# A hybrid decoder trunk on one core: parameter transfers held back behind the first unit of weights, and skip factors loaded as rows

## The chip, the core and the metric

The kernel runs as one program on one core of one Trainium2 chip. The metric is the device time of one execution in microseconds (us). The time before is the median of three runs.

## The reference, cut to what matters

Two decoder layers over 256 tokens of width 1024, all in float32. Each layer adds a mixer and a feed-forward part to the running activations, each behind an RMSNorm. The mixer projects the normed activations with `w_in` (1024 x 3592) into three groups: a short gated convolution, a state-space group (SSD, eight heads of 64) and a conformer convolution of 31 taps. What touches the change is the SSD group and the order of its small parameters:

```python
proj = h @ w_in
dt = softplus(s_dt + dt_bias)          # s_dt: 8 of the columns of proj
a = -exp(a_log)
y_s = ssd_chunked(xh, dt, a, ...)
y_s = y_s + d_skip[:, None] * xh       # one factor per head and layer
y_s = gated_rmsnorm(y_s, s_z, ssd_norm_w)
```

The feed-forward part is a dense SwiGLU in layer 0 and, in layer 1, two of eight SwiGLU experts per token, chosen by a router. A last RMSNorm ends the work.

## The kernel before, in words

Weights come from memory as a list of units, each a tile `raw` of about 2 MB, through a ring of four buffers (later nine). `Stream.load_upto` issues their transfers on SyncE's queue (SP below), in the order of the list. A unit is used in pieces: for each piece ScalarE rounds it to `whi` (line 235), VectorE forms the rest `wlo` (line 236), and TensorE runs three matmuls per block of 128 rows (`mm3`, lines 409 to 411: `whi` with `xh`, `whi` with `xl`, `wlo` with `xh`). Pieces are made four ahead of their use. Unit 0, 512 columns of `w_in`, is loaded in four quarters of 512 KB, one per piece (the branch `FINE`, line 200), each with runs of 512 bytes; the other mixer units come in one transfer (line 202) with runs of 2 KB.

At the start ACT loads one row tile, and SP issues `x` in four quarters (line 277), then the four quarters of unit 0, then eight rows of parameters of layer 0 (`prow_load(0)`, line 302), then units 1, 2, 3. TensorE transposes `x` (line 333); ScalarE and VectorE copy it to `xT` and split it, scaled, into `xh` and `xl` (lines 418, 419).

GpSimd (POOL) issues the other small parameters on its own queue as soon as the program starts, lines 306 to 317: `dtb` and `alg` (the same 16 floats to every partition), `wdt` for each layer (eight columns of `w_in`: 1024 runs of 32 bytes), two row sets into `prow2`, `dsk` in two halves (64 partitions x 8 single floats, 4 bytes each, picked by stride so that each half of the partitions holds the factors of its heads), eight rows of layer 1 (`prow_load(1)`) and the router weights `wr`. Their users are: `na` = exp of `alg` (line 529, ScalarE), `wdh` and `wdl`, the split of `wdt` (lines 371 and 372), `dtv` (line 556), `ys` with `dsk` (line 634), and `load_rest` (from line 377) with `prow2`, `prow1` and `wr`.

SP issues in the written order (`MANUAL`); ScalarE, VectorE and TensorE do so at the very start, and later a scheduler sets their order. An engine runs its instructions in that order: one that waits holds all behind it.

Of the kernel before, what the change touches and what calls it, by code (L numbers as in the profile page):

```python
# [8 lines left out]
F32 = mybir.dt.float32  # L9
# [6 lines left out]
P = 128  # L16
T = 256
D = 1024
KD = D // P
# [14 lines left out]
HC = DFE // 2  # L34
LW = HC // 4
HB = HC // P
MANUAL = {mybir.EngineType.SP}


@with_exitstack  # L40
def hybrid_decoder(
# [6 lines left out]
    nc = tc.nc  # L48
    ACT, DVE, PE, POOL = nc.scalar, nc.vector, nc.tensor, nc.gpsimd
# [7 lines left out]
    work = t1.enter_context(tc.tile_pool(name="work", bufs=1))  # L57
    ctx.enter_context(tc.manual_schedule(engines=MANUAL))

# [7 lines left out]
    units = []  # L67
# [181 lines left out]
    ws = Stream()  # L249
# [32 lines left out]
    prow2 = work.tile([12, P], F32, name="prow2")  # L282
    COL = {}
    wdt = work.tile([P, 2, KD, 8], F32, name="wdt")
    wdh = work.tile([P, 2, KD, 8], F32R, name="wdh")
    wdl = work.tile([P, 2, KD, 8], F32R, name="wdl")
    dtb = work.tile([P, 2, 8], F32, name="dtb")
    alg = work.tile([P, 2, 8], F32, name="alg")
    dsk = work.tile([P, 2, 4], F32, name="dsk")
    wr = const.tile([P, KD, E], F32, name="wr")  # L290

    def bcast(ap, dims):
        return bass.AP(tensor=ap.tensor, offset=ap.offset, ap=[[0, P]] + dims)

    def prow_load(i):
        r = 0
        for nm, ap, n in (("conf", conv_conf_w[i].rearrange("k c -> (k c)"), 62),
                          ("conv_ssd", conv_ssd_w[i].rearrange("k c -> (k c)"), 32),
                          ("ssd_b", conv_ssd_b[i], 8), ("norm_mix", norm_mix[i], 8), ("norm_ffn", norm_ffn[i], 8),
                          ("conv_a", conv_a_w[i].rearrange("k c -> (k c)"), 6),  # L300
                          ("conf_b", conv_conf_b[i], 2), ("ln_g", conf_ln_g[i], 2)):
            (nc.gpsimd if i else nc.sync).dma_start(prow[i][r:r + n], ap.rearrange("(r c) -> r c", c=P))
            COL[nm] = r
            r += n

    nc.gpsimd.dma_start(dtb, bcast(dt_bias, [[8, 2], [1, 8]]))
    nc.gpsimd.dma_start(alg, bcast(a_log, [[8, 2], [1, 8]]))
    for i in range(2):
        nc.gpsimd.dma_start(wdt[:, i], w_in[i, :, 2304:2312].rearrange("(k p) n -> p k n", p=P))
    nc.gpsimd.dma_start(prow2[0:4], conf_ln_b.rearrange("l (r c) -> (l r) c", c=P))  # L310
    nc.gpsimd.dma_start(prow2[4:12], ssd_norm_w.rearrange("l (r c) -> (l r) c", c=P))
    for h in range(2):
        nc.gpsimd.dma_start(dsk[h * 64:(h + 1) * 64],
                            bass.AP(tensor=d_skip.tensor, offset=d_skip.offset + h,
                                    ap=[[0, 64], [8, 2], [2, 4]]))
    prow_load(1)
    nc.gpsimd.dma_start(wr, moe_router[0].rearrange("(k p) n -> p k n", p=P))

    pc = [work.tile([P, P], F32, name=f"pc{i}") for i in range(2)]
    pc2 = work.tile([P, 12], F32, name="pc2")  # L320
# [2 lines left out]
    def col(i, nm, j):  # L323
        if nm == "ln_b":
            return pc2[:, 2 * i + j:2 * i + j + 1]
        if nm == "ssd_norm":
            return pc2[:, 4 + 4 * i + j:5 + 4 * i + j]
        if nm == "norm_mix" and i == 0:
            return pcn[:, j:j + 1]
        return pc[i][:, COL[nm] + j:COL[nm] + j + 1]  # L330
# [85 lines left out]
    def scaled_split(i, nm, j, xh, xl):  # L416
        w = col(i, nm, j)
        ACT.activation(xh[:, j], xT[:, j], AF.Copy, scale=w)
        DVE.scalar_tensor_tensor(xl[:, j], xT[:, j], w, xh[:, j].bitcast(F32), op0=OP.mult, op1=OP.subtract)
# [396 lines left out]
    for j in range(KD):  # L816
        if j == 1:
            ws.make_upto(1)
            prow_load(0)
        scaled_split(0, "norm_mix", j, xh, xl)  # L820
    start_pe.close()
    ws.make_upto(2)
# [325 lines left out]
    for q in range(NS):  # L1148
        e, h = divmod(q, 2)
# [178 lines left out]
```

## Time and profile before

| | |
|---|---|
| three runs | 1308.5, 1310.47, 1310.91 us; median 1310.47 |
| profiled execution | 1314.7 us, span 1312.8 us |
| TensorE busy | 1218.4 us (93%) |
| VectorE, ScalarE, GpSimd busy | 464.2, 266.0, 12.2 us |
| transfers | 424.01 MB, mean 323 GB/s |
| GpSimd's queue (software) | 688 packets, 0.72 MB, 0.7% of 16 engines' span |
| SyncE's queue | 90452 packets, 421.09 MB, 80.9% |

The span is the profiled stretch; the execution's own time is 1.9 us longer. Busy shares are averages over stages with different limits, so the page alone does not say what a microsecond at the start is worth. In the page's 40 slices TensorE stands at nine tenths or more in nearly all but the first, where it has four.

### The profile page before, as it was taken

The page shows a single profiled execution, that of the slowest core. Times are in us where ns is not written, and L with a number is a line of the kernel's source. Part 1 is how long each engine was busy: PE and PEld are TensorE (multiplying, and loading weights), DVE is VectorE, ACT ScalarE, POOL GpSimd, SP SyncE. Part 2 cuts the span into 40 slices and gives each one's busy share as a digit, 9 for nine tenths or more (in the row PEclk, how much of TensorE's full clock was granted, in tenths as well). Part 3 has the DMA queues.
Part 4 walks back from the last instruction along what each step waited for, and adds up shares of the span by engine and source line. Part 5 has one row for each costly group of instructions (what it writes and reads, how often), then busy time and mean ns, then how long its engine had stood idle before and what let it go on. Part 6 is the DMA issues. An engine that isn't in the chain of part 4 may idle for free. (4 is left out here: it accounts for less than half of the span.)

```text
span 1312.8 us, 28824 instructions
## 1 busy us (share of the span) xinstructions
PE 1218.4 (93%) x12994; PEld 792.9 (60%) x12994; DVE 464.2 (35%) x948; ACT 266.0 (20%) x446; POOL 12.2 (1%) x34
## 2 busy tenths in 40 slices
PE   4999999999999899999999999999999997897794
PEld 3997999999998734454444544545635533343242
DVE  3898765556898411101201111111020121020213
ACT  3671544444670300000000000100000000000001
POOL 3000000000000000000000000000000000000000
PEclk9999999999999899999999999999999999999997
DMA  7852465555252799999999999999999999999993
GB/s 157 300 193 65 161 205 183 191 193 193 97 185 73 316 371 384 381 411 420 422 417 422 419 410 422 417 422 420 418 422 418 418 422 417 421 420 418 420 357 121
DMA packets 91303, 424.01 MB, mean 323 GB/s; under 512 B 4590, under 2 KB 33493, under 8 KB 83476
## 3 DMA queue, kind: packets, MB, share of 16 engines
q1 hardware_dynamic: 90452, 421.09, 80.9%
q0 software_dynamic: 688, 0.72, 0.7%
q8 instruction: 122, 2.00, 0.6%
q14 instruction: 25, 0.20, 0.0%
q10 hardware_dynamic: 16, 0.00, 0.0%
HBM read 420.74 MB, written 1.05 MB: 321 GB/s over the span
## 5 line engine op out<-in xcount | busy, mean ns | idle before, releaser
L1034 PE MATMUL psA<-raw,xe 128*32 128x448 f32 x5024 | 485.8, 541 | 25.3 <-DMA raw<-in_moe_w_gate_dram 9.7
L1034 PEld LDWEIGHTS psA<-raw,xe 128*32 128x32 f32 x5024 | 180.7, 110 | 319.8 <-issue 286.5
L1078 PE MATMUL psB<-raw,ht 128*32 128x256 f32 x4296 | 240.7, 380 | 18.8 <-DMA raw<-in_moe_w_down_dram 10.7
L1078 PEld LDWEIGHTS psB<-raw,ht 128*32 128x32 f32 x4296 | 151.6, 110 | 108.5 <-issue 18.3
L409 PE MATMUL psB<-xh,whi 128*128 128x256 f32 x608 | 173.1, 285 | 0.0
L411 PE MATMUL psB<-xh,wlo 128*128 128x256 f32 x608 | 172.5, 284 | 0.0
L410 PE MATMUL psB<-xl,whi 128*128 128x256 f32 x608 | 172.2, 283 | 0.0
L236 DVE TENSOR_TENSOR wlo<-raw,whi 128x1024 fp32r<-128x1024 f32 x110 | 134.0, 1223 | 59.8 <-ACT whi L235 59.7
L235 ACT CAST whi<-raw 128x1024 fp32r<-128x1024 f32 x110 | 114.8, 1048 | 114.3 <-PE psB L410 51.9
L1054 ACT ACTIVATE sg<-psA 128x448 f32<-128x448 f32 x48 | 24.5, 542 | 476.7 <-PE psA L1034 466.7
L409 PEld LDWEIGHTS psB<-xh,whi 128*128 128x128 f32 x608 | 116.6, 192 | 0.7 <-issue 0.7
L411 PEld LDWEIGHTS psB<-xh,wlo 128*128 128x128 f32 x608 | 116.5, 192 | 0.2
L410 PEld LDWEIGHTS psB<-xl,whi 128*128 128x128 f32 x608 | 116.5, 192 | 0.1
L1066 DVE TENSOR_TENSOR pr<-psA,sg 128x448 f32<-128x448 f32 x48 | 43.0, 922 | 203.5 <-PE psA L1034 203.5
L1104 DVE STREAM_TRANSPOSE yt<-yc 128x256 f32<-128x256 f32 x24 | 9.7, 431 | 234.7 <-ACT yc L1102 234.4
L693 PE MATMUL psA<-yf,raw 128*128 128x256 f32 x256 | 62.2, 399 | 5.4 <-ACT yf L733 3.0
L693 PEld LDWEIGHTS psA<-yf,raw 128*128 128x128 f32 x256 | 49.7, 199 | 13.5 <-ACT yf L733 3.5
L1018 DVE COPY xe<-psC 128x384 f32<-128x384 f32 x8 | 4.5, 558 | 149.0 <-PE psC L1016 149.0
L540 DVE SCALAR_TENSOR_TENSOR conv<-gp,pc,conv 128x256 f32<-128x256 f32 x120 | 50.8, 476 | 0.0
L410 PE MATMUL psA<-al,whi 128*128 128x256 f32 x176 | 49.8, 283 | 0.0
L411 PE MATMUL psA<-ah,wlo 128*128 128x256 f32 x176 | 49.7, 282 | 0.0
L409 PE MATMUL psA<-ah,whi 128*128 128x256 f32 x176 | 49.3, 280 | 0.0
(285 smaller groups left out, 879.7 us busy)
## 6 DMA issues: line engine op xcount, KB each, us to landing
raw<-in_moe_w_gate_dram SPq DMA_DIRECT2D x64, 1792.0 KB, 25.5
raw<-in_moe_w_up_dram SPq DMA_DIRECT2D x64, 1792.0 KB, 23.9
raw<-in_moe_w_down_dram SPq DMA_DIRECT2D x30, 2048.0 KB
raw<-in_moe_w_down_dram SPq DMA_DIRECT2D x30, 1536.0 KB, 24.4
raw<-in_w_in_dram SPq DMA_DIRECT2D x9, 2048.0 KB, 14.0
raw<-in_ffn_w_gate_dram SPq DMA_DIRECT2D x11, 1024.0 KB, 5.4
raw<-in_ffn_w_up_dram SPq DMA_DIRECT2D x11, 1024.0 KB, 8.0
raw<-in_ffn_w_down_dram SPq DMA_DIRECT2D x5, 2048.0 KB, 9.0
```

Source lines behind the costliest of these rows:

```text
L235: ACT.copy(hi, raw)
L236: DVE.tensor_tensor(lo, raw, hi.bitcast(F32), op=OP.subtract)
L409: PE.matmul(ps, lhsT=hi, rhs=xh, start=start, stop=False, **kw)
L410: PE.matmul(ps, lhsT=hi, rhs=xl, start=False, stop=False, **kw)
L411: PE.matmul(ps, lhsT=lo, rhs=xh, start=False, stop=stop, **kw)
L540: DVE.scalar_tensor_tensor(conv[:, c], src, w, conv[:, c], op0=OP.mult, op1=OP.add)
L693: PE.matmul(acc[j][:, a], lhsT=raw[:, k, w], rhs=yf[b][:, k], start=(b + k == 0 and a == 0), stop=(b + k == 4), skip_group_check=True)
L1034: PE.matmul(banks[t][32 * j:32 * j + 32, 0:LW], lhsT=x[:, k, 32 * t:32 * t + 32], rhs=raw[:, k % 2, LW * j:LW * j + LW], start=(k == 0), s ...
L1054: ACT.activation(sg[:, t], bg[t][:, 0:LW], AF.Silu)
L1066: DVE.tensor_tensor(pr[:, t], by(bu[t][:, 0:LW]), by(sg[:, t]), op=OP.mult)
L1078: PE.matmul(psd[t // 2][32 * j:32 * j + 32, 256 * (t % 2):256 * (t % 2) + 256], lhsT=ht[:, t, b], rhs=w[:, j], start=(h == 0 and b == 0 an ...
L1104: DVE.transpose(yt[:, :, 32 * t:32 * t + 32], yc[:, t].rearrange("p (n c) -> p n c", c=32))
```

## The change

`MANUAL` now holds GpSimd too, so that its instructions run in the written order. All of its parameter transfers move into a function `late_params`, called after SP's `prow_load(0)` has been written. It begins with a GpSimd copy, `gate`, that reads the last element of unit 0's tile: GpSimd cannot go on before the last quarter of unit 0 has landed. `alg` now stands ahead of `dtb`. The two strided loads of `dsk` become one load of 16 floats to every partition (`dsall`) and, at the end, two GpSimd copies that pick every second column.

```diff
-MANUAL = {mybir.EngineType.SP}
+MANUAL = {mybir.EngineType.SP, mybir.EngineType.Pool}
...
+    dsall = work.tile([P, 2, 8], F32, name="dsall")
...
-    nc.gpsimd.dma_start(dtb, bcast(dt_bias, [[8, 2], [1, 8]]))
-    nc.gpsimd.dma_start(alg, bcast(a_log, [[8, 2], [1, 8]]))
-    for i in range(2):
-        nc.gpsimd.dma_start(wdt[:, i], w_in[i, :, 2304:2312].rearrange("(k p) n -> p k n", p=P))
...
-    for h in range(2):
-        nc.gpsimd.dma_start(dsk[h * 64:(h + 1) * 64],
-                            bass.AP(tensor=d_skip.tensor, offset=d_skip.offset + h,
-                                    ap=[[0, 64], [8, 2], [2, 4]]))
-    prow_load(1)
-    nc.gpsimd.dma_start(wr, moe_router[0].rearrange("(k p) n -> p k n", p=P))
+    def late_params():
+
+        gate = work.tile([P, 1], F32, name="gate")
+        POOL.tensor_copy(gate, ws.raw[0][:, KD - 1, units[0]["n"] - 1:units[0]["n"]])
+        nc.gpsimd.dma_start(alg, bcast(a_log, [[8, 2], [1, 8]]))
+        nc.gpsimd.dma_start(dtb, bcast(dt_bias, [[8, 2], [1, 8]]))
+        for i in range(2):
+            nc.gpsimd.dma_start(wdt[:, i], w_in[i, :, 2304:2312].rearrange("(k p) n -> p k n", p=P))
+        nc.gpsimd.dma_start(dsall, bcast(d_skip, [[8, 2], [1, 8]]))
...
+        prow_load(1)
+        nc.gpsimd.dma_start(wr, moe_router[0].rearrange("(k p) n -> p k n", p=P))
+        for h in range(2):
+            POOL.tensor_copy(dsk[h * 64:(h + 1) * 64],
+                             dsall[h * 64:(h + 1) * 64].rearrange("p l (c h) -> p l c h", h=2)[:, :, :, h])
...
             prow_load(0)
+            late_params()
```

The order on GpSimd at the start, before (a row with x2 stands for two instructions):

```order
L259 IOTA jp 128x128
L279 IOTA before 128x64
L306 DMA dtb<-in_dt_bias_dram 128x16
L307 DMA alg<-in_a_log_dram 128x16
L309 DMA wdt<-in_w_in_dram 128x8x8 x2
...
L313 DMA dsk<-in_d_skip_dram 64x8x1 x2
...
L317 DMA wr<-in_moe_router_dram 128x8x8
L844 DMA wffn<-in_norm_ffn_dram 128x1024
```

And now, where lines below the change have moved by up to six:

```order
L259 IOTA jp 128x128
L279 IOTA before 128x64
L310 COPY gate<-raw 128x1
L311 DMA alg<-in_a_log_dram 128x16
L312 DMA dtb<-in_dt_bias_dram 128x16
L314 DMA wdt<-in_w_in_dram 128x8x8 x2
L315 DMA dsall<-in_d_skip_dram 128x16
...
L319 DMA wr<-in_moe_router_dram 128x8x8
L321 COPY dsk<-dsall 64x8 x2
L850 DMA wffn<-in_norm_ffn_dram 128x1024
```

The gate stands ahead of every transfer, and the two picking copies behind the last of them.

The order on ScalarE from the copies of `x` to unit 1's first piece, before (the `whi` rows ahead of `wdh` are unit 0's four pieces, the one behind it is unit 1's):

```order
L356 COPY xT<-psA 128x4x128
L529 ACTIVATE nega<-alg 128x16
L356 COPY xT<-psA 128x4x128
L418 ACTIVATE xh<-xT,pcn 128x256
L235 CAST whi<-raw 128x1024
L418 ACTIVATE xh<-xT,pcn 128x256 x7
L235 CAST whi<-raw 128x1024
L424 ACTIVATE sq<-xT 128x2048
L235 CAST whi<-raw 128x1024 x2
L371 CAST wdh<-wdt 128x64 x2
L235 CAST whi<-raw 128x1024 x4
```

And now:

```order
L361 COPY xT<-psA 128x4x128 x2
L423 ACTIVATE xh<-xT,pcn 128x256
L235 CAST whi<-raw 128x1024
L423 ACTIVATE xh<-xT,pcn 128x256 x7
L235 CAST whi<-raw 128x1024
L429 ACTIVATE sq<-xT 128x2048
L235 CAST whi<-raw 128x1024 x2
L534 ACTIVATE nega<-alg 128x16
L376 CAST wdh<-wdt 128x64 x2
L235 CAST whi<-raw 128x1024 x4
```

`nega` has moved from between the copies of `x` to a place behind unit 0's four casts and ahead of `wdh`; unit 1's casts stand behind both. The order on SP, VectorE and TensorE is unchanged.

## Rows read from the trace of the kernel before

**Rows 1.** Stretches: length, busy us of each engine (count), granted clock, DMA share, GB/s.

```profile
30.00:100.00 70.00, 69.94 (x580) 66.95 (x579) 66.19 (x151) 47.35 (x82) 0.00 (x0) 1.00 0.70 248
440.00:700.00 260.00, 250.81 (x3015) 126.22 (x3017) 43.24 (x125) 20.47 (x41) 0.00 (x0) 0.99 0.99 403
```

**Rows 2.** TensorE's waits from 25 to 410 us, in total, times, longest.

```profile
PE psA L693 <- ACT yf L733: 1.5, 1, 1.5
...
PE psC L333 <- DVE rc L400: 0.2, 1, 0.2
```

**Rows 3.** The timeline's start: start us, us, engine, line, work, idle before it.

```profile
2.63 18.23 SPq L200 DMA_DIRECT2D raw<-in_w_in_dram  x4
3.42 2.31 PE L333 MATMUL psA<-ident,x_tok 128*128 128x128 f32 x8 [0.54 <-DMA x_tok<-in_x_dram]
9.09 1.97 PE L333 MATMUL psA<-ident,x_tok 128*128 128x128 f32 x8 [3.37 <-DMA x_tok<-in_x_dram]
10.73 0.51 ACT L418 ACTIVATE xh<-xT,pcn 128x256 fp32r<-128x256 f32 x1
21.35 1.04 ACT L235 CAST whi<-raw 128x1024 fp32r<-128x1024 f32 x1 [10.11 <-DMA raw<-in_w_in_dram]
22.45 0.58 PE L409 MATMUL psA<-xh,whi 128*128 128x256 f32 x1 [11.38 <-ACT whi L235]
23.71 0.58 PE L411 MATMUL psA<-xh,wlo 128*128 128x256 f32 x1 [0.46 <-DVE wlo L236]
25.96 0.23 SPq L302 DMA_DIRECT2D prow<-in_conf_ln_g_dram  x1
26.77 10.74 SPq L202 DMA_DIRECT2D raw<-in_w_in_dram  x4
34.56 3.93 ACT L235 CAST whi<-raw 128x1024 fp32r<-128x1024 f32 x4 [4.43 <-DMA raw<-in_w_in_dram]
38.72 0.39 PE L411 MATMUL psB<-xh,wlo 128*128 128x256 f32 x1
```

**Rows 4.** GpSimd's timeline at the start, same columns.

```profile
1.03 0.23 POOL L279 IOTA before<- 128x64 f32 x1
1.38 0.69 POOL L306 DMA_DIRECT2D dtb<-in_dt_bias_dram  x1
2.06 0.55 POOL L307 DMA_DIRECT2D alg<-in_a_log_dram  x1
2.61 1.78 POOL L309 DMA_DIRECT2D wdt<-in_w_in_dram  x2
21.68 0.94 POOL L317 DMA_DIRECT2D wr<-in_moe_router_dram  x1
```

**Rows 5.** Tiles `wdt` (two rows) and `dsk`, transfer `wr`: landing us from issue.

```profile
L371 ACT CAST wdh<-wdt x2: 241/241/241, 29.7 to 29.9; 128x64 fp32r<-128x64 f32 x2
DMA to landing us min/median/max: 8.5/9.8/11.0
...
DMA to landing us min/median/max: 11.0/12.9/14.8
...
wr<-in_moe_router_dram POOLq DMA_DIRECT2D x1, 32.0 KB, 5.2
```

**Rows 6.** Stretches at the start, columns as in the first group.

```profile
3.00:6.00 3.00, 2.23 (x8) 1.43 (x8) 0.83 (x4) 0.59 (x1) 3.00 (x5) 1.00 0.47 122
14.00:18.00 4.00, 0.00 (x0) 0.00 (x0) 0.00 (x0) 0.00 (x0) 2.00 (x4) 1.00 0.77 23
22.00:24.00 2.00, 1.09 (x3) 0.80 (x4) 1.57 (x3) 2.00 (x6) 0.62 (x1) 1.00 1.07 278
24.00:28.00 4.00, 4.00 (x20) 4.00 (x20) 3.56 (x8) 4.00 (x7) 0.00 (x0) 1.00 0.28 54
28.00:34.00 6.00, 6.00 (x52) 6.00 (x52) 4.81 (x11) 2.13 (x4) 0.00 (x0) 1.00 0.98 359
```

**Rows 7.** Tile `prow`: duration min/median/max, first and last start us.

```profile
L333 PE MATMUL psC<-ident,prow x2: 270/286/301, 38.0 to 64.2; 128*128 128x128 f32 x2
```

More of the change, by code (lines that the diff above doesn't have):

```diff
@@ L304, in prow_load @@
             r += n
-    nc.gpsimd.dma_start(dtb, bcast(dt_bias, [[8, 2], [1, 8]]))
-    nc.gpsimd.dma_start(alg, bcast(a_log, [[8, 2], [1, 8]]))
-    for i in range(2):
-        nc.gpsimd.dma_start(wdt[:, i], w_in[i, :, 2304:2312].rearrange("(k p) n -> p k n", p=P))
-    nc.gpsimd.dma_start(prow2[0:4], conf_ln_b.rearrange("l (r c) -> (l r) c", c=P))
-    nc.gpsimd.dma_start(prow2[4:12], ssd_norm_w.rearrange("l (r c) -> (l r) c", c=P))
-    for h in range(2):
-        nc.gpsimd.dma_start(dsk[h * 64:(h + 1) * 64],
-                            bass.AP(tensor=d_skip.tensor, offset=d_skip.offset + h,
-                                    ap=[[0, 64], [8, 2], [2, 4]]))
-    prow_load(1)
-    nc.gpsimd.dma_start(wr, moe_router[0].rearrange("(k p) n -> p k n", p=P))
+    def late_params():
[6 more added lines that the diff above has]
+        nc.gpsimd.dma_start(dsall, bcast(d_skip, [[8, 2], [1, 8]]))
+        nc.gpsimd.dma_start(prow2[0:4], conf_ln_b.rearrange("l (r c) -> (l r) c", c=P))
+        nc.gpsimd.dma_start(prow2[4:12], ssd_norm_w.rearrange("l (r c) -> (l r) c", c=P))
+        prow_load(1)
[3 more added lines that the diff above has]
+                             dsall[h * 64:(h + 1) * 64].rearrange("p l (c h) -> p l c h", h=2)[:, :, :, h])
     pc = [work.tile([P, P], F32, name=f"pc{i}") for i in range(2)]
```

## The prediction

> **What bounds the kernel now.** I read the stretches first, then TensorE's waits, then the start of the timeline, and last the transfers at the start. The stretch table puts the engines in the order TensorE, its weight loads, VectorE, ScalarE, GpSimd. From 30 to 100 us TensorE is busy 69.94 of 70 us [rows 1], and its waits from 25 to 410 us are six, together 3.6 us, none on a transfer; the first and the last of the six stand in the list [rows 2]. From 440 us the sixteen DMA engines are busy 0.99 and deliver 403 GB/s [rows 1]: the experts' stage is held by its weights, whose loading begins when the mixer of layer 1 ends on TensorE. So nothing after about 25 us is tied to an absolute time. Whatever moves TensorE's first dense work moves all that follows by the same amount.
>
> The start is different. TensorE transposes half of x at 3.42 us, the other half, which lands late, at 9.09 us, and then idles 11.38 us until 22.45 us, because ScalarE's first cast waited 10.11 us for unit 0, until 21.35 us [rows 3]. SP needed 18.23 us to issue unit 0's four quarters [rows 3]: its queue was backed up. The transfers ran at 122 GB/s from 3 to 6 us and at 23 GB/s from 14 to 18 us, though megabytes were waiting; at 22 to 24 us unit 0's 512-byte runs went at 278 GB/s, and unit 1's 2 KB runs later at 359 GB/s [rows 6]. In the bad stretches GpSimd's small transfers were on their way: two for `wdt` that took 8.5 and 11.0 us, two for `dsk` that took 11.0 and 14.8 us [rows 5]. That they hold the big ones up is my reading of the coincidence, not something a row states.
>
> **The change, step by step.** All against the profiled execution of 1314.7 us, whose span is 1312.8; it lies 4.2 us above the median of 1310.47, and I take the gain off the median.
>
> *The start without GpSimd's transfers.* The first quarter of x has landed by 3.42 us [rows 3]; the other three, 0.79 MB at 359 GB/s [rows 6], take 2.2 us: x is complete at 5.6. From the late half's arrival (9.09) to the end of the first `xh` (10.73 + 0.51) were 2.15 us, from the cast's start to the first matmul 1.10 us [rows 3]: TensorE starts at 5.6 + 2.15 + 1.10 = 8.85 us instead of 22.45, a shift of **13.6 us**. Unit 0, 2.10 MB at 278 GB/s [rows 6], takes 7.5 us and is complete at 13.1; its first quarter is there at 7.5, before ScalarE wants it at 7.75. The bounds: with x landing as late as now, TensorE starts at 9.09 + 2.15 + 1.10 = 12.3 (shift 10.1); an empty queue cannot give more than the 13.6 by much.
>
> *What is late next.* A dense marker is TensorE's first matmul with unit 1's `wlo`, at 38.72 us now [rows 3]. With nothing in its way it would come at 38.72 - 13.6 = 25.1 us. Ahead of it three things must have happened.
>
> Unit 1: SP's last parameter row waited for unit 0's last quarter until 25.96, unit 1's issue came 0.81 us later, its cast 7.79 us after that [rows 3]. That is 13.1 + 0.8 + 7.8 = 21.7 us, and the marker 2.36 us behind the cast's start (21.35 to 23.71 [rows 3]) at 24.1: in time, if unit 1 is not slowed.
>
> `alg` and `wdt`: ScalarE runs in order, and `nega` and the two `wdh` casts now stand directly ahead of unit 1's casts, so a late `wdt` holds unit 1's casts, VectorE's `wlo` behind them and TensorE. GpSimd's gate opens at 13.1. Its copy of one column is in no row; I take the small 0.23 us iota [rows 4], bounds 0 and 1 us. Then the issues of `alg` 0.55, `dtb` 0.69 and the first `wdt` 0.89 [rows 4]: the second `wdt` is issued at 15.5. It then takes 5.2 us, as `wr` did, which has the same shape, at a time when unit 0 was flowing at 278 GB/s [rows 5, 6], or 11.0 us, as this transfer itself did beside a choked queue [rows 5]. I take 11.0, since three more big units will be behind SP's queue: 26.5 us. The last `wdh` cast takes 0.24 [rows 5], and the marker comes 2.36 later: **29.1 us**. TensorE so loses 4.0 of the 13.6 us in a wait that is new.
>
> *The sum.* 38.72 - 29.1 = 9.6 us gained. 1310.47 - 9.6 = **1300.9 us** (the profiled execution would be 1305.1).
>
> *Costed at nothing.* `dsk` is used far later, and its two copies on GpSimd, some 0.2 us each by the iota, hide behind the whole first mixer. The last of GpSimd's list, `wr`, was issued 20.3 us after the first (1.38 to 21.68 [rows 4]); from 13.35 that is 33.7, landed by 39; `load_rest` runs around 64.2 [rows 7], hence not before 50. If that cover of 11 us were gone, VectorE would wait there. Unit 4's transfer also waits for the gate's read, which is over long before. SP's own order and its waits shift with unit 0.
>
> **A rule against it.** The rows show bulk going at 23 GB/s beside the small transfers and 359 without them [rows 6]. The Trainium skill ("DMA: Bandwidth & Descriptors", section "Queues, rings and completion order") says that each DMA engine takes turns between queues packet by packet, so that small packets put off now take their turns from unit 1 to 3 in place of unit 0. By it alone the cost would be moved, not removed, and the sum would be the third rival's.
>
> **Rivals.**
>
> 1. *The small transfers cost little beside 2 KB runs* (0.22). `wdt` lands in 5.2 us like `wr`, at 20.7; unit 1 at 21.7 is the later, the marker is at 25.1 and the whole 13.6 us stay: 1296.9. For it: `wr` beside 278 GB/s. Against: `wdt` now.
> 2. *x's late half is not GpSimd's doing* (0.13). Then x is complete at 9.09, unit 0 at 16.6, and everything on GpSimd is 3.5 us later: marker at 32.6, gain 6.1: 1304.4. For it: at 3 to 6 us the DMA engines were busy only 0.47 [rows 6], which no queue explains.
> 3. *Unit 1 pays what unit 0 paid* (0.15). Unit 0 was complete at 25.96 instead of 13.1: 12.9 us lost. The second `wdt`, issued at 3.5, landed at 14.5; the later `dsk`, issued after 4.39 and 14.8 on its way, not before 19.2 [rows 4, 5]: at least 4.7 us go with `dsk`, or, if none of the loss is its doing, nothing. Unit 1 then comes 8.2 to 12.9 us late, at 29.9 to 34.6, the marker at 32.3 to 37.0: gain 1.7 to 6.4, less a slow restart. After its long idle TensorE did 20 matmuls in 4 us, then 52 in 6, with the granted clock at 1.00, its upper level of 2.4 GHz, in both rows [rows 6]: at the later pace the 20 take 2.3, so a second slow start costs 1.7. In all 0 to 6.4, middle 3.2: 1307.3.
> 4. *Slower: GpSimd's queue starves behind the units* (0.05). Units 1 to 3, 6.3 MB at 359 GB/s [rows 6], hold the engines from 13.9 to 31.4 us. If `wdt` is served only after them, in 5.2 to 11.0 us, it lands at 36.6 to 42.4 and the marker at 39.2 to 45.0: 0.5 to 6.3 us slower, and 1.7 more with a slow restart, about 1314.5. It decides when `wdt` lands after 36.1 us, 20.6 us behind its issue. Against it: the longest landing in the trace is 14.8 [rows 5].
>
> **The numbers.** My forecast, 1300.9, has 0.45. The range takes in rivals 1 and 2 and half of 3, with the runs' spread of 1.2 us about the median: 1295.8 to 1307.5. Outside are the worse half of 3 and rival 4. A difference of 0.2%, 2.6 us, is about what a measurement can tell from no change: faster by more 0.88 (forecast, 1, 2 and half of 3), within it 0.07, slower 0.05.
>
> **What would show it.** TensorE's first matmul with `whi` near 9 us (12 by rival 2); SP issuing unit 0 in well under 18 us; GpSimd's first transfer near 13 us; ScalarE waiting for `wdt` at `wdh`, or for unit 1 at the next cast, a few us about 26; no small gap later that was not there. I am wrong if unit 0 still arrives near 20 us with GpSimd's queue silent (another cause of the choke), or if TensorE waits 10 us or more ahead of unit 1.

## The result, and the profile after

| | before | changed |
|---|---|---|
| runs beside each other | 1310.69 us median (1308.5 to 1313.4, 4 runs) | 1303.99 us median (1302.87 to 1305.26, 4 runs) |
| profiled execution, span | 1314.7, 1312.8 us | 1305.26, 1303.3 us |
| ratio | | 0.9938, 95% interval 0.9921 to 0.9956 |

The change makes the kernel 6.7 us faster, where 9.6 were forecast. Two later comparisons gave the same: 0.9942 (0.9925 to 0.9959) and 0.9943 (0.9926 to 0.996). The start of the changed kernel, from its timeline (start us, us, engine, line, work, idle before it and what ended it; lines lie up to 6 further down than before), answers to [rows 3, 4]:

```profile
2.62 6.03 SPq L200 DMA_DIRECT2D raw<-in_w_in_dram  x4
6.32 1.97 PE L338 MATMUL psA<-ident,x_tok 128*128 128x128 f32 x8 [0.35 <-DMA x_tok<-in_x_dram]
8.96 1.04 ACT L235 CAST whi<-raw 128x1024 fp32r<-128x1024 f32 x1 [0.50 <-DMA raw<-in_w_in_dram]
10.06 0.58 PE L414 MATMUL psA<-xh,whi 128*128 128x256 f32 x1 [1.77 <-ACT whi L235]
13.95 1.22 DVE L236 TENSOR_TENSOR wlo<-raw,whi 128x1024 fp32r<-128x1024 f32 x1
14.13 1.09 POOL L310 COPY gate<-raw 128x1 f32<-128x1 f32 x1 [12.87 <-DMA raw<-in_w_in_dram]
14.69 13.77 SPq L202 DMA_DIRECT2D raw<-in_w_in_dram  x4
16.38 1.80 POOL L314 DMA_DIRECT2D wdt<-in_w_in_dram  x2
25.24 0.48 ACT L376 CAST wdh<-wdt 128x64 fp32r<-128x64 f32 x2 [4.05 <-DMA wdt<-in_w_in_dram]
25.52 0.23 DVE L377 TENSOR_TENSOR wdl<-wdt,wdh 128x64 fp32r<-128x64 f32 x1 [4.89 <-ACT wdh L376]
25.66 0.42 DVE L433 TENSOR_TENSOR sq<-sq 128x256 f32<-128x256 f32 x1
26.13 1.01 PE L441 MATMUL psC<-ones,sq 128*128 128x1 f32 x4 [4.03 <-DVE sq L433]
26.60 2.94 ACT L235 CAST whi<-raw 128x1024 fp32r<-128x1024 f32 x3 [0.89 <-DMA raw<-in_w_in_dram]
32.36 0.28 PE L416 MATMUL psB<-xh,wlo 128*128 128x256 f32 x1
```

Read it as a chain. SP issues unit 0 in 6.03 us instead of 18.23, x is complete at 6.32, and TensorE's first dense matmul stands at 10.06 instead of 22.45: a shift of 12.4 us. Then comes a wait that no row before has. The first of the two `wdt`, let go by the gate, lands at 25.2 and the second by 25.5; ScalarE casts them; VectorE forms the first `wdl`; and only behind it, in VectorE's order, stands the last sum of squares of the tokens (`sq`). TensorE needs that sum **inside unit 0** and stands still for 4.03 us. The marker, the first matmul with unit 1's `wlo`, comes at 32.36 instead of 38.72: of 12.4 us 6.4 are left. Before, VectorE had the same order, and it cost nothing, since `wdt` had long landed:

```profile
32.94 0.22 DVE L372 TENSOR_TENSOR wdl<-wdt,wdh 128x64 fp32r<-128x64 f32 x1
33.07 0.42 DVE L428 TENSOR_TENSOR sq<-sq 128x256 f32<-128x256 f32 x1
```

TensorE's waits from 25 to 410 us (in total, times, longest), beside [rows 2], hold one that is new, and the stretches (columns as in [rows 1]) show what follows it:

```profile
PE psC L441 <- DVE sq L433: 4.0, 1, 4.0
PE psA L698 <- DVE yf L711: 2.4, 2, 1.2
PE psA L698 <- ACT yf L738: 1.5, 1, 1.5
```

(The 2.4 us for `yf` are two waits of 1.2; before, the second lay just beyond 410 us.)

```profile
3.00:6.00 3.00, 2.23 (x8) 1.43 (x8) 0.16 (x2) 0.59 (x1) 0.00 (x0) 1.00 0.79 236
18.00:22.00 4.00, 4.00 (x35) 3.90 (x33) 2.62 (x3) 0.22 (x1) 2.81 (x6) 1.00 1.04 299
26.00:32.00 6.00, 5.87 (x27) 5.87 (x28) 4.76 (x21) 3.71 (x4) 3.32 (x7) 0.51 1.06 387
```

From 3 to 6 us the transfers run at 236 GB/s instead of 122 [rows 6]. From 26 to 32 us TensorE is busy, but does 27 matmuls with the granted clock at 0.51, its lower level of 1.2 GHz, where 52 fitted into six such us before [rows 6]. So 12.4 us are gained, 4.0 lost in the wait, and the remaining 2.0 (12.4 - 4.0 - 6.4) at the lower clock behind it.

In this pair the start moves the rest as a block as far as layer 1: the first matmul of its mixer output stands 6.48 us earlier, and the difference of the medians is 6.7. The two profiled executions differ by 9.4 all the same. Before, then changed, on TensorE's timeline:

```profile
405.56 1.89 PE L693 MATMUL psA<-yf,raw 128*128 128x256 f32 x8
...
432.93 5.41 PE L693 MATMUL psA<-yf,raw 128*128 128x256 f32 x16 [1.52 <-ACT yf L733]
...
452.81 6.26 PE L1016 MATMUL psC<-G,hn 128*128 128x96 f32 x32 [3.50 <-DVE G L931]
```

```profile
399.08 1.89 PE L698 MATMUL psA<-yf,raw 128*128 128x256 f32 x8
...
426.44 3.72 PE L698 MATMUL psA<-yf,raw 128*128 128x256 f32 x16 [1.52 <-ACT yf L738]
...
444.63 5.41 PE L1022 MATMUL psC<-G,hn 128*128 128x96 f32 x32 [3.50 <-DVE G L937]
```

The same 16 matmuls behind the same wait of 1.52 us take 5.41 us in one and 3.72 in the other, the next block 6.26 and 5.41: 2.5 us. That is not the change's doing. In the third profile of the changed kernel the 16 take 5.41 us too, with the granted clock at 0.66 there, and in that profile the last 96 matmuls of the experts take 1.7 us longer than before as well (the rows stand at the end of the experiments):

```profile
422.15 5.41 PE L698 MATMUL psA<-yf,raw 128*128 128x256 f32 x16 [1.52 <-ACT yf L738]
```

From the mixer's first matmul to the end of the span the fourteen profiles below take 904 to 909 us, the three of the changed kernel 904.2, 904.2 and 907.8. That is why the start is judged by its markers and the gain by medians.

### The profile page after: what moved, and what is told of

It is laid out like the page before. It is cut to its first block, busy times and chain, and to the rows that moved or that the text cites. A ratio compares the mean times of both kernels' runs of the same rounds, so it can differ in the third digit from the quotient of the medians.

```text
span 1303.3 us, 28827 instructions
## 1 busy us (share of the span) xinstructions
PE 1218.1 (93%) x12994; PEld 791.7 (61%) x12994; DVE 464.1 (36%) x948; ACT 266.3 (20%) x446; POOL 12.8 (1%) x36
## 5 line engine op out<-in xcount | busy, mean ns | idle before, releaser
L1084 PE MATMUL psB<-raw,ht 128*32 128x256 f32 x4296 | 241.8, 380 | 19.4 <-DMA raw<-in_moe_w_down_dram 14.1
## 6 DMA issues: line engine op xcount, KB each, us to landing
raw<-in_moe_w_gate_dram SPq DMA_DIRECT2D x64, 1792.0 KB, 25.7
```

Of the source, the lines that this page charges most:

```text
L1084: PE.matmul(psd[t // 2][32 * j:32 * j + 32, 256 * (t % 2):256 * (t % 2) + 256], lhsT=ht[:, t, b], rhs=w[:, j], start=(h == 0 and b == 0 an ...
```

## The experiments

Times of start in us from one profile each; "unit 1" is from its issue on SP to ScalarE's first cast of it (in brackets where the cast waited for something else); "mixer" is layer 1's first mixer-output matmul.

| kernel | first dense matmul | unit 1 | marker | mixer | profiled | median |
|---|---|---|---|---|---|---|
| before | 22.45 | 7.8 | 38.72 | 405.56 | 1314.7 | 1310.7 |
| changed | 10.06 | 11.9 | 32.36 | 399.08 | 1305.3 | 1304.0 |
| changed, again | 10.31 | 12.4 | 32.66 | 398.15 | 1304.3 | 1304.0 |
| changed, third | 9.73 | (11.3) | 29.67 | 394.78 | 1304.6 | 1305.1 |
| rows alone | 14.31 | (7.7) | 30.84 | 397.69 | 1306.1 | 1303.7 |
| gate alone | 10.42 | (11.7) | 30.11 | 396.92 | 1308.0 | 1310.4 |
| gate alone, again | 10.49 | 19.2 | 37.74 | 407.05 | 1316.1 | one run |
| both casts held | 10.30 | 11.4 | 29.55 | 395.92 | 1304.6 | 1307.6 |
| `wdl` held | 9.55 | 12.0 | 29.52 | 396.35 | 1302.5 | 1308.1 |
| `wdt` first, held | 10.95 | 12.2 | 31.22 | 400.42 | 1311.4 | 1305.6 |
| broadcasts last | 10.69 | 8.4 | 31.55 | 400.98 | 1309.6 | one run |
| split, gate on unit 0 | 10.93 | 9.7 | 28.93 | 395.99 | 1305.8 | 1306.2 |
| split, gate on unit 1 | 11.03 | 7.7 | 27.82 | 395.05 | 1300.9 | 1302.7 |
| the same, again | 10.87 | 7.6 | 27.81 | 395.04 | 1301.4 | 1303.2 |

The medians come from four comparisons, in which the kernel before had 1310.7 (the first run of the changed kernel), 1311.8 or 1312.0 us. Markers and medians do not go together throughout: against the runs before beside them both held kernels and the split with its gate on unit 0 gain 3.9 to 5.8 us in the median, where the mixer in their one profile stands 9.2 to 9.6 us earlier, and the changed kernel's third profile has the earliest mixer of all without the best time. A marker shows what happens at the start; what it is worth at the end only the medians show.

### Either half of the change alone

**Rows alone**: the skip factors as rows with GpSimd's copies, but no gate; everything is issued at the program's start. The order is that of before, with `dtb` ahead of `alg` and `dsall` in `dsk`'s old place, which the excerpt below does not show.

```diff
-        gate = work.tile([P, 1], F32, name="gate")
-        POOL.tensor_copy(gate, ws.raw[0][:, KD - 1, units[0]["n"] - 1:units[0]["n"]])
...
+    late_params()
...
-            late_params()
```

> Skip factors as rows and picked on GpSimd, without the gate: GpSimd's transfers start with the program as before, in the old order, only the two strided loads of dsk are gone. Theory (the gate does most of it, dsk a part of it): unit 0's first cast comes 3 to 6 us before the 21.35 us of the kernel before, and the time falls by 3 to 6 us. Rival (dsk's 4-byte runs are the whole choke): the first cast comes at 9 to 11 us and the time falls by 9 or more, since nothing is late. Rival (dsk does nothing to the start): cast near 21 us, same time within 1.5 us.

Measured: 1303.74 us (1301.14 to 1306.1), ratio 0.9937 (0.9921 to 0.9953): **the whole gain of the change.** From its timeline:

```profile
2.62 9.69 SPq L200 DMA_DIRECT2D raw<-in_w_in_dram  x4
8.66 1.97 PE L338 MATMUL psA<-ident,x_tok 128*128 128x128 f32 x8 [2.53 <-DMA x_tok<-in_x_dram]
14.31 0.58 PE L414 MATMUL psA<-xh,whi 128*128 128x256 f32 x1 [3.68 <-ACT whi L235]
26.21 2.95 ACT L235 CAST whi<-raw 128x1024 fp32r<-128x1024 f32 x3 [4.22 <-PE psA L415]
```

Without the strided loads unit 0 is issued in 9.69 us instead of 18.23 and TensorE starts 8.1 us earlier, though every other small transfer is still in its way. Those cost the start 4.3 us (14.31 against 10.06), and x's late half with it: 8.66 here, 9.09 before [rows 3], 6.32 with GpSimd silent. But since `wdt` is early, no engine waits later (unit 1's cast waits for TensorE, not for a transfer), and 7.9 of the 8.1 us arrive at the marker.

**Gate alone**: the gate and the moved transfers, with `dsk`'s two strided loads kept among them.

```diff
-        nc.gpsimd.dma_start(dsall, bcast(d_skip, [[8, 2], [1, 8]]))
+        for h in range(2):
+            nc.gpsimd.dma_start(dsk[h * 64:(h + 1) * 64],
+                                bass.AP(tensor=d_skip.tensor, offset=d_skip.offset + h,
+                                        ap=[[0, 64], [8, 2], [2, 4]]))
...
-        for h in range(2):
-            POOL.tensor_copy(dsk[h * 64:(h + 1) * 64],
-                             dsall[h * 64:(h + 1) * 64].rearrange("p l (c h) -> p l c h", h=2)[:, :, :, h])
```

> The gate alone: all of GpSimd's transfers behind unit 0, dsk in its two strided loads as before the change. Theory: TensorE starts at 10 us as in the changed kernel, wdt stands ahead of dsk in the queue and lands near 25.5 us as there, so the time is that of the changed kernel within 1.5 us. Rival (4-byte runs choke the units behind them): unit 1's first cast comes 3 us or more later than its 26.6 us in the changed kernel, and 3 us or more of the gain go.

> A second look at the gate alone with the strided loads kept, whose profile showed a start 8.6 us ahead of before but whose median did not. If its start differs from run to run (the strided loads meet units 1 and 2 at another moment), unit 1's or unit 2's cast stands elsewhere than at 26.3 and 39.5 us, by 2 us or more, and the first mixer matmul of layer 1 at 399 us or later; if the start is the same within 0.5 us, the lost time lies after it, in the granted clock at the two later places.

Measured: 1310.41 us (1307.34 to 1316.73, 12 runs), ratio 0.9994 (0.9979 to 1.0009): **nothing.** The two profiles, at 1308.0 and 1316.1 us, show what varies. A stretch and ScalarE's casts, first profile, then second:

```profile
26.00:30.00 4.00, 3.62 (x21) 3.13 (x19) 3.20 (x15) 3.86 (x5) 1.85 (x4) 0.57 0.75 24
```

```profile
26.29 3.88 ACT L235 CAST whi<-raw 128x1024 fp32r<-128x1024 f32 x4
39.51 2.00 ACT L235 CAST whi<-raw 128x1024 fp32r<-128x1024 f32 x2 [2.16 <-DMA raw<-in_w_in_dram]
```

```profile
26.00:30.00 4.00, 3.86 (x21) 3.63 (x19) 2.08 (x13) 0.24 (x1) 1.99 (x4) 0.57 1.11 15
```

```profile
34.15 3.88 ACT L235 CAST whi<-raw 128x1024 fp32r<-128x1024 f32 x4 [7.82 <-DMA raw<-in_w_in_dram]
```

While `dsk` is on its way, all transfers together move 24 and 15 GB/s; before it was 23, from 14 to 18 us [rows 6]. The choke goes wherever these two loads go. In the first profile unit 1 had just landed and unit 2 paid; in the second unit 1 was caught and came 19.2 us after its issue: the marker was only 1.0 us earlier than before, and layer 1's mixer 1.5 us later. In both TensorE also waited for `sq`, 1.8 and 2.3 us. This is the third rival of the prediction, complete, but for a kernel that keeps the strided loads. In the queues' rows (packets, MB, share of sixteen engines' time in the first 60 us) these loads make 32 packets more on GpSimd's queue than the row in their place; the first fence is the gate alone, the second the changed kernel:

```profile
q0 software_dynamic: 544, 0.19, 14.5%
```

```profile
q0 software_dynamic: 512, 0.20, 4.7%
```

The Trainium skill ("DMA: Bandwidth & Descriptors", section "Rules for kernel authors") says that a strided last dimension becomes one descriptor per element and should be made contiguous. The trace agrees with the advice: fewer bytes, three times the engines' time. The rule that the prediction weighed, turns packet by packet, would have the cost moved; for the gate alone the medians agree with it, and for the whole change they don't, because the change also takes the worst packets away.

### The stall inside unit 0

Two kernels make VectorE unable to place `wdl` early. A factor `one` (the norm's factor times 0 plus 1) is read where the cast is made, so that the work can't be ordered ahead of the norm. **Both casts held** does it for ScalarE's `wdh`, on which `wdl` depends; **`wdl` held** for VectorE alone.

```diff
+            DVE.tensor_scalar(one, r[:, 0:1], 0.0, 1.0, op0=OP.mult, op1=OP.add)
...
-        ACT.copy(wdh[:, i], wdt[:, i])
+        ACT.activation(wdh[:, i], wdt[:, i], AF.Copy, scale=one)
```

```diff
-        DVE.tensor_tensor(wdl[:, i], wdt[:, i], wdh[:, i].bitcast(F32), op=OP.subtract)
+        DVE.scalar_tensor_tensor(wdl[:, i], wdt[:, i], one, wdh[:, i].bitcast(F32), op0=OP.mult, op1=OP.subtract)
```

> The changed kernel with the split of wdt (two casts on ScalarE, two subtractions on VectorE) held until the layer's reciprocal norm is there, by a factor of one made from it: neither stands ahead of VectorE's last sum of squares or of unit 1's first cast any more. Theory (4.0 us of TensorE's wait inside unit 0, and a slow restart of some 2 us behind it, come from wdl standing ahead of the last sum): the wait for sq is gone, no slow matmuls near 27 us; what stays is unit 1's landing at 26.5 us, so the first matmul with unit 1's wlo comes at about 29 us instead of 32.4, and the time is about 1300.6, 3.4 us under the changed kernel. Rival (unit 1's landing is what counts and the wait for sq hid in it): the marker stays near 32 us and the time at 1304.

> The changed kernel with one thing undone: `wdl`'s subtraction reads a factor made from the norm, so that it can't stand ahead of unit 0's last sum of squares on VectorE; ScalarE's casts of `wdt` stay where they are, ahead of unit 1's. Theory A (VectorE's order alone made the stall inside unit 0): TensorE no longer waits for `sq`, its pace stays at the upper clock from 26 us on, and its wait moves to unit 1's first cast, as the prediction had it: marker with unit 1's `wlo` at 29 to 30 us instead of 32.4 to 32.7, 9 to 10 us earlier than before; the first mixer matmul of layer 1 near 396 us. Rival (the restart costs the same wherever the wait stands): the wait moves but the marker stays at 31.5 us or later.

In both the wait for `sq` is gone. With `wdl` held, ScalarE's and TensorE's timelines and the stretch that answers to the one above:

```profile
25.97 3.89 ACT L235 CAST whi<-raw 128x1024 fp32r<-128x1024 f32 x4 [0.36 <-DMA raw<-in_w_in_dram]
27.06 0.38 PE L415 MATMUL psB<-xh,whi 128*128 128x256 f32 x1 [1.64 <-ACT whi L235]
28.96 0.54 PE L415 MATMUL psB<-xh,whi 128*128 128x256 f32 x1 [1.40 <-ACT whi L235]
```

```profile
26.00:32.00 6.00, 3.51 (x15) 2.94 (x16) 4.96 (x7) 4.54 (x6) 4.53 (x7) 0.75 1.06 382
```

TensorE now finishes unit 0 and waits 3.0 us for unit 1, in two pieces, at the place where the prediction had its wait; the marker stands at 29.52, 0.4 from the 29.1 of the forecast. VectorE's order alone made the stall inside unit 0; without it the marker comes 2.8 us earlier than in the changed kernel's first profile, 0.5 of them from the first matmul. But it is only 0.15 us ahead of the third, in which the first `wdt` landed 1.7 us sooner and the stall was half as long:

```profile
PE psC L441 <- DVE sq L433: 2.0, 1, 2.0
```

So the order is shown to make the stall, and what it costs hangs on when the first `wdt` lands. Waiting for unit 1 remains when `wdh` is out of the way, since unit 1 itself lands only at 25.97.

The medians do not follow: 1307.57 us (ratio 0.9963, 0.9946 to 0.9979) and 1308.09 (0.9966, 0.9953 to 0.9978), by some 3 us worse than the changed kernel with its later start, though the intervals of the ratios overlap (0.9926 to 0.996 for the changed kernel beside `wdl` held). With `wdl` held the profiled execution, 1302.45, is the fastest of seven; the other six lie at 1306.1 to 1308.7, with mean granted clocks of 0.982 to 0.987 against its 0.989. Where those six lost their time no profile shows, so this stays open.

### What makes unit 1 late

Unit 1 took 7.8 us before and 11.9 in the changed kernel. Two kernels sort the suspects. **`wdt` first, held** issues `wdt` at the program's start and leaves the rest behind the gate, as in the changed kernel. **Broadcasts last** does the same, but GpSimd issues the parameter rows and `wr` first and `dtb`, `alg` and `dsall` at the end.

```diff
+    for i in range(2):
+        nc.gpsimd.dma_start(wdt[:, i], w_in[i, :, 2304:2312].rearrange("(k p) n -> p k n", p=P))
...
         POOL.tensor_copy(gate, ws.raw[0][:, KD - 1, units[0]["n"] - 1:units[0]["n"]])
...
         nc.gpsimd.dma_start(wr, moe_router[0].rearrange("(k p) n -> p k n", p=P))
+        nc.gpsimd.dma_start(dtb, bcast(dt_bias, [[8, 2], [1, 8]]))
+        nc.gpsimd.dma_start(alg, bcast(a_log, [[8, 2], [1, 8]]))
+        nc.gpsimd.dma_start(dsall, bcast(d_skip, [[8, 2], [1, 8]]))
```

> As the one before, and wdt's two transfers are issued at the program's start, ahead of the gate; no engine waits for them early. Theory (wdt's 32-byte runs are the main part of the choke): unit 0's first cast comes at 13 us or later instead of 9, and the time is 3 us or more above the one before. Rival (the broadcast loads and dsk choked the start, not wdt): the start stays at 9 to 10 us, unit 1 lands by 24 us since wdt is out of its way, and the time is 2 us or more below the one before.

> `wdt` at the start and its casts held, gate on unit 0, but GpSimd issues the norm rows, the parameter rows of layer 1 and `wr` first and the three broadcast rows (`dtb`, `alg`, the skip factors) last. If the broadcasts are what makes unit 1 late, its cast comes about 8 us after its issue, near 23 to 24 us; if the row transfers and `wr` do it, unit 1 stays at 12 us after its issue, near 27 us. VectorE has to wait for `dtb` later than before, which may cost some us after 35 us; the look is at unit 1 alone.

With `wdt` gone from its side unit 1 still takes 12.2 us, so `wdt` is not what delays it; at the start `wdt` costs about 1 us (10.95 against 9.73 to 10.31). With the broadcasts last it takes 8.4. The stretch in which unit 1 flows, first with the broadcasts ahead of the rows, then behind them:

```profile
18.00:22.00 4.00, 4.00 (x35) 4.00 (x35) 3.96 (x7) 0.52 (x2) 2.25 (x5) 1.00 1.05 278
```

```profile
18.00:22.00 4.00, 4.00 (x36) 4.00 (x35) 3.79 (x9) 0.07 (x1) 2.45 (x6) 1.00 1.06 390
```

So the three loads that give the same 16 floats to every partition, 8 KB each, take most of the 4 us; the ten row transfers ahead of them take under 1. What `wr` costs this does not show, since it was issued only 1.2 us before unit 1's cast. Both kernels pay elsewhere: in the first TensorE waits 3.7 us for unit 1, in the second `alg`, late now, holds ScalarE and with it TensorE for 4.1, and both reach layer 1's mixer later than the changed kernel.

### A further version

**Split** issues `wdt`, `dtb` and `alg` at the start, with their first uses held as above, and gates the rest. Once the gate reads the last element of unit 1, once that of unit 0.

```diff
+    for i in range(2):
+        nc.gpsimd.dma_start(wdt[:, i], w_in[i, :, 2304:2312].rearrange("(k p) n -> p k n", p=P))
+    nc.gpsimd.dma_start(dtb, bcast(dt_bias, [[8, 2], [1, 8]]))
+    nc.gpsimd.dma_start(alg, bcast(a_log, [[8, 2], [1, 8]]))
...
-        POOL.tensor_copy(gate, ws.raw[0][:, KD - 1, units[0]["n"] - 1:units[0]["n"]])
+        POOL.tensor_copy(gate, ws.raw[1][:, KD - 1, units[1]["n"] - 1:units[1]["n"]])
...
-            late_params()
...
+    ws.load_upto(2)
+    late_params()
```

> `wdt`, `dtb` and `alg` are transferred at the start, the casts of `wdt` and the exponential of `alg` are held until the norm's factor exists, and the gate for all the rest (skip rows, norm rows, `wr`) stands behind unit 1's last element in place of unit 0's. Theory A (only the strided 4-byte loads of `dsk` choke the start; the small transfers let loose behind unit 0 are what makes unit 1 late, 11.9 us for 7.8): the first dense matmul at 11 to 12 us, unit 1's cast about 8 us after its issue, near 23 us, TensorE's marker with unit 1's `wlo` at 27 to 29 us, no wait of TensorE over 1 us before 40 us: 10 to 11.5 us faster than before, near 1299. Theory B (unit 1 is late for a reason of its own, whatever GpSimd's queue does): unit 1's cast at 26 us or later, marker 31 to 32 us, 6 to 7.5 us faster, as the changed kernel. Theory C (`dtb` and `alg`, or `wdt`, choke the start as `dsk` did): the first dense matmul after 14 us, and unit 1 then without a wait; about 8 us faster.

> As the variant before, `wdt`, `dtb` and `alg` at the start, but the gate for the rest stays on unit 0's last element. Theory A: unit 1 is again beside small transfers (skip rows, norm rows, `wr`): its cast 10 us or more after its issue, near 25 us, TensorE waits 2 to 4 us for it, marker 29 to 31 us, 7 to 9 us faster than before and 2 to 3 behind the variant with the gate on unit 1. If unit 1 now comes in 8 us as well, what made it late was `wdt`, `alg` or `dtb`, and the two variants agree within 1 us. Theory B: both variants alike, unit 1 at 26 us or later.

The split kernel with the later gate, its timeline and two stretches:

```profile
23.38 0.18 POOL L315 COPY gate<-raw 128x1 f32<-128x1 f32 x1 [18.94 <-DMA raw<-in_w_in_dram]
23.40 2.94 ACT L235 CAST whi<-raw 128x1024 fp32r<-128x1024 f32 x3 [4.99 <-DMA raw<-in_w_in_dram]
27.82 0.39 PE L418 MATMUL psB<-xh,wlo 128*128 128x256 f32 x1
```

```profile
18.00:22.00 4.00, 4.00 (x36) 4.00 (x35) 3.97 (x5) 0.41 (x1) 0.00 (x0) 1.00 1.05 402
26.00:32.00 6.00, 6.00 (x49) 5.41 (x48) 5.89 (x12) 3.75 (x9) 3.89 (x8) 1.00 1.05 333
```

Theory A held for the start, and not for the time, which it had near 1299. Unit 1 comes 7.7 us after its issue, at 402 GB/s; TensorE waits for nothing from its first dense matmul to 32 us beyond the 0.5 us of the first `wlo`, the clock stays at 1.00, and 10.9 of the 11.4 us gained at the first matmul arrive at the marker. With the gate on unit 0, one broadcast (`dsall`) beside it, unit 1 takes 9.7 us and the marker is 1.1 later.

Gate on unit 1: 1302.72 us (1300.91 to 1305.21), ratio 0.9941 (0.9923 to 0.9959). Gate on unit 0: 1306.2, 0.9962 (0.9951 to 0.9973). Whether the first of them beats the changed kernel by more than the spread, a second comparison of both was to show.

> The changed kernel itself once more, beside the two variants on one chip. All theories: first dense matmul near 10.1 us, VectorE's last sum of squares of unit 0 behind `wdl` and TensorE waiting 4 us for it, first matmul with unit 1's `wlo` near 32.4 us; 6 to 7 us faster than before, ratio about 0.994 to 0.995. Should the stall for the sum of squares be missing in this profile, my reading that VectorE's order makes it would fall.

> The best start so far once more, to see whether it beats the changed kernel by more than the spread of the runs. By the profiles the start is 3 us ahead of the changed kernel; the time after the last mixer takes one of few values by the granted clock at two places (16 `yf` matmuls in 3.72 or 5.41 us near 424, the last 96 matmuls of the experts in 5.4 or 7.1 us), so single runs differ by up to 5 us. Expected: marker with unit 1's `wlo` at 27.8, first mixer matmul of layer 1 at 395, median 1300.5 to 1303, 1 to 3 us below the changed kernel.

> The changed kernel beside these on the same chip: median 1303 to 1305, marker 32.4 to 32.7, the stall of 4 to 5 us for the last sum of squares again. For the two places with a granted clock of their own: with both at the upper level the profiled time is near 1304 to 1305, with one lower 2.4 us more.

The split kernel: 1303.2 us (1300.44 to 1304.18), ratio 0.9927 (0.9912 to 0.9943), its marker and mixer the same to 0.01 us in both profiles. The changed kernel beside it: 1304.01 in the first comparison, 1305.09 in the second. So the split one's median is ahead by 1.3 and 1.9 us, but the ratios (0.9941 against 0.9942, then 0.9927 against 0.9943) have intervals that overlap: that it is faster is not shown. The changed kernel's own start varies more, since its stall hangs on when the first `wdt` lands: 4.0, 4.8 and 2.0 us in three profiles. In the third the first dense matmul, 9.73, and the marker, 29.67, are the best of the three, and the profiled time is no better, because both later places ran partly at the lower clock (granted 0.66 and 0.79). Its last block of 96 matmuls of the experts, then that of before:

```profile
1274.40 7.07 PE L1084 MATMUL psB<-raw,ht 128*32 128x256 f32 x96 [2.48 <-PEq L1096]
```

```profile
1286.05 5.39 PE L1078 MATMUL psB<-raw,ht 128*32 128x256 f32 x96 [2.44 <-PEq L1090]
```

## Why the prediction was right, and where its terms were off

- **Direction and range** held: 1303.99 lies between 1295.8 and 1307.5. The size was 2.9 us too good.
- **The start**: forecast 8.85 us for the first dense matmul, measured 10.06, a shift of 12.4 for 13.6. x was complete at 6.32 and not 5.6: I had taken 359 GB/s, the rate of 2 KB runs [rows 6], and 236 flowed from 3 to 6 us; and the first cast waited 0.50 us more for unit 0. Rival 2, x late for its own reasons, falls: with GpSimd silent its late half comes 2.8 us earlier.
- **The gate**: the copy was costed at 0.23 us and took 1.09, just beyond its bound of 1. Unit 0 was complete at 14.1 instead of 13.1.
- **`wdt`**: forecast to land at 26.5, issued at 15.5 and 11.0 on its way; the second was issued at 17.3, was 8.2 on its way and landed by 25.5. That the landing was so near is luck: the later gate and the slower issues added 1.8, the shorter way took 2.8 back. 8.2 lies about midway between the 11.0 of its old choked transfer and the 5.2 of `wr`, so neither row was its price; rival 1, which took 5.2, falls.
- **The step that failed** is "What is late next". I listed ScalarE's order, unit 1's casts behind `wdh`, and forgot VectorE's: the first `wdl` stands ahead of the last sum of squares, which TensorE needs inside unit 0. The 4.0 us that I gave the new wait were right by chance; it came earlier, inside unit 0, and the lower clock behind it took 2.0 more, which I had put into rival 3 only. Holding `wdl` alone puts a wait where the prediction had it and the marker at 29.52, but that wait, 3.0 us, ends with unit 1 itself, which landed 0.4 us behind the last `wdh`.
- **Unit 1** was to be in time "if it is not slowed". It was, by 4.1 us; at 25.7 `wdh` would have held its cast nearly as long, which is why this cost little. Rival 3 was right that unit 1 pays something of what unit 0 paid: the broadcasts' part of it, not `dsk`'s.
- **Where the gain comes from** was read wrongly in emphasis. I credited the gate and left `dsk`'s share between nothing and 4.7 us or more (rival 3). Rows alone give 8.1 us at the first matmul and the whole gain in the median; the gate adds 4.3 at the start, and by the marker 6.0 are lost again.
- **No small gap later** held: the other waits from 25 to 410 us are those of before.

## What to carry to other kernels

Look first at the shape of small transfers and then at their moment: two loads of single floats by stride choked everything beside them for several us wherever they stood, and turning them into rows was worth more than moving all the rest. When a transfer is put off, go through every in-order engine that touches it and name what stands behind it there, not only on the engine that uses it first. And give up a little at the start for a transfer that is needed soon: the split kernel begins 1 us later than the changed one and is 4.5 us ahead at unit 1 by the first profiles, 1.9 against the changed kernel's best; that it is faster at the end is not shown.

## What the runs showed of the hardware

**GpSimd's one-column copy waits for VectorE.** The gate took 1.09 us from 14.13, and its end at 15.22 falls on that of VectorE's `wlo` subtraction, 13.95 + 1.22 = 15.17; the split kernel's gate met VectorE idle and took 0.18. In all ten profiles with the gate on unit 0 it took 0.93 to 1.20 us and ended 0.03 to 0.05 us behind such a subtraction. The Trainium skill ("SBUF — State Buffer", section "SBUF: two separate sides") says that of a VectorE instruction with two inputs in SBUF and a GpSimd instruction that reads SBUF, the one that starts first holds the ports that they share for its whole length, and the other waits. These rows agree.

**The same wait, two clocks.** After 4.03 us of standing still TensorE ran at 0.51; in the split kernel, with no such wait, the same stretch stayed at 1.00. Before, after 11.38 us of idling, the rows give 1.00 from 24 us on [rows 3, 6], and yet the matmuls came as slowly: 20 in the 4 us from 24 to 28, against 27 in six us at 0.51. So at the program's start the granted clock alone does not show a slow stretch; the count of matmuls does. Behind one and the same wait of 1.52 us near 425 us it was sometimes at 1.00 and sometimes at 0.66, and nothing in these rows tells which it will be. Over the profiles the time after layer 1's mixer differed by up to 5 us, as much as the difference between most of these kernels; these two places account for part of it.
